# Local attention on one core: two slots for q and k, three for v and three for the output, and later requests for q and k

## The chip, the cores and the metric

The kernel runs on one core of one Trainium2 chip. The metric is the time of one execution on the device in microseconds (us). Before the change it is 954.06 us (median of 3 runs, 953.35 to 955.11); with the fourth run of the round that timed the change it is 954.44 us, and three later calls gave medians of 953.93 to 954.1 us for the same kernel. The profiler's span is about 1.8 us shorter than the time of the same execution (951.8 us beside 953.58 us).

Names in the profile: PE does the matrix products (PEld loads its weights), DVE and ACT do the vector and scalar work, GpSimd (POOL in the profile's lines) and SP issue transfers here. A DMA transfer is moved by the core's 16 DMA engines in packets, and it has landed when all of them have done their share.

## The reference

Attention in windows of 64 rows; a row attends to its own window alone.

```python
B, S, D, W = 4, 4096, 1536, 64
q_w = q.reshape(B, nw, W, D)            # k and v likewise; all float32
logits = einsum('bnwd,bnud->bnwu', q_w, k_w) * D ** -0.5
attn = exp(logits - logits.max(-1)); attn /= attn.sum(-1)
out = einsum('bnwu,bnud->bnwd', attn, v_w)
```

q, k, v and the output have 100.66 MB each, 402.7 MB in all. Every byte crosses between HBM and the core once.

## The kernel before

The 16,384 rows are cut into 32 units of 512 rows. The loads cast float32 to float16, and all loads and all stores but the last three small ones are issued by GpSimd on one queue. The last unit, unit 31, is cut into three parts (256, 128, 128 rows), so that the kernel ends with small pieces of work.

```python
AHEAD = 2
SLOTS = 4
...
units = [Unit(i * UR, [(0, 4, 2)]) for i in range(N - 1)]
units.append(Unit((N - 1) * UR, [(0, 2, 2), (2, 3, 1), (3, 4, 1)]))
inp = ctx.enter_context(tc.tile_pool(name="inp", bufs=AHEAD + 1))   # q, k, v: three slots each
outp = ctx.enter_context(tc.tile_pool(name="outp", bufs=2))
...
def load(u, i, name):
    ...
    nc.gpsimd.dma_start(out=dst, in_=rows(src, u.first[i], hi - lo, r))

def load_all(u):
    for i in range(len(u.parts)):
        for name in "qkv":
            load(u, i, name)
...
def values(u, i, h, et, last):
    if not hasattr(u, "o"):
        u.o = outp.tile([P, SLOTS, D], FP32, tag="out_sb", name="out_sb")
    ...                                  # row sums, products, each block scaled into u.o by ACT or DVE
            if last:
                nc.sync.dma_start(out=of[u.first[i] : u.first[i] + P, sl], in_=dst)

def store(u, i):
    lo, hi, R = u.parts[i]
    nc.gpsimd.dma_start(out=rows(of, u.first[i], hi - lo, R), in_=slots(u.o, lo, hi, R))

for ui, u in enumerate(units):
    if ui + AHEAD < N:
        load_all(units[ui + AHEAD])
    n = ui - 12
    if 1 <= n <= 15 and n != 8:          # 14 small loads that nothing uses
        w = 128 + 4 * n
        nc.gpsimd.dma_start(out=probe[:n, n, :w], in_=qf[0:n, :w])
    for i in range(len(u.parts)):
        last = ui == N - 1 and i == len(u.parts) - 1
        for h, et in scores(u, i):       # transposes of q and k, products, exp
            values(u, i, h, et, last)
        if not last:
            store(u, i)
```

A request waits in GpSimd's program order: for its slot to come free, and for one of eight transfers in flight to land. So a load that waits holds up the store behind it. In the timeline of before the first eight loads are issued by 6.4 us, and the ninth at 12.45 us, when the first has landed.

The softmax here doesn't subtract the row's maximum and nothing guards it: scores larger than these inputs give would overflow.

## Time and profile before

| | before |
|---|---|
| time, median of 3 runs | 954.06 us |
| span of the profiled execution | 951.8 us |
| PE, DVE, ACT busy | 70%, 45%, 45% |
| packet time on the 16 DMA engines, main queue | 100.6% of 16 spans |
| HBM traffic over the span | 423 GB/s |

The first lines are from the profile's page of before: DMA busy tenths in 40 slices, and the queues with packets, MB and the share of 16 engines' span that their packets took (a little over 100%, so the times of packets overlap).

```profile
DMA  9999999999999999999999999999999999999996
...
q0 software_dynamic: 27824, 250.96, 100.6%
q8 instruction: 44, 0.72, 0.3%
```

The DMA engines are full until the last slice.

The table by stretches of before follows, with busy time of each engine (and instructions), the granted clock of PE, the mean DMA share and GB/s.

```profile
core 0: us, PE busy (x) PEld busy (x) DVE busy (x) ACT busy (x) POOL busy (x), PEclk, DMA share, GB/s
150.00:440.00 290.00, 208.87 (x1712) 134.09 (x1711) 129.88 (x147) 132.82 (x188) 24.46 (x40) 0.87 1.02 270
...
930.00:935.00 5.00, 2.47 (x6) 0.80 (x6) 1.32 (x2) 1.37 (x2) 0.00 (x0) 0.50 0.70 297
935.00:940.00 5.00, 4.40 (x39) 3.09 (x37) 2.56 (x5) 1.61 (x3) 0.54 (x1) 0.72 0.54 229
940.00:945.00 5.00, 2.84 (x34) 2.03 (x34) 1.94 (x4) 3.35 (x6) 0.54 (x1) 1.00 0.63 259
945.00:951.80 6.80, 1.51 (x10) 0.57 (x10) 0.92 (x2) 2.00 (x5) 0.00 (x0) 0.72 0.49 188
```

In the middle the share is 1.02. From 930 us on it falls to about a half: the tail is not full. GpSimd's timeline of before (start, duration, what; in brackets the idle time before it and what ended it) shows why.

```profile
853.10 0.72 POOL L214 DMA_DIRECT2D out_dram<-out_sb  x1 [8.50 <-DVE out_sb L207]
858.98 0.54 POOL L79 DMA_DIRECT2D q<-in_q_dram  x1 [5.16 <-DMA k<-in_k_dram]
...
906.18 0.53 POOL L79 DMA_DIRECT2D v<-in_v_dram  x1 [3.11 <-DMA q<-in_q_dram]
910.13 0.71 POOL L214 DMA_DIRECT2D out_dram<-out_sb  x1 [3.43 <-ACT out_sb L205]
913.81 0.72 POOL L214 DMA_DIRECT2D out_dram<-out_sb  x1 [2.96 <-ACT xk L141]
937.60 0.54 POOL L214 DMA_DIRECT2D out_dram<-out_sb  x1 [23.07 <-DVE xq L141]
```

Between 859 and 906 us the nine small loads of unit 31 go out one by one. Unit 29's output was complete at 882.2 us (the end of DVE's last block), but its store stands behind them and goes out at 910.13. Unit 31 uses the same output slot as unit 29, so it has to wait. The list of waits of before (engine and line, what it waited for, us in total, times, longest):

```profile
DVE out_sb L207 <- DMA out_dram<-out_sb: 48.0, 19, 13.6
ACT out_sb L205 <- DMA out_dram<-out_sb: 30.0, 16, 14.1
```

The longest waits, 13.6 and 14.1 us, end at 931.8 us in the timeline, when that store has landed.

### The profile page before, as it was taken

What the parts mean: (1) busy time and instruction counts of PE and PEld (TensorE: products, weight loads), DVE (VectorE), ACT (ScalarE), POOL (GpSimd) and SP (SyncE); (2) the same over time, 40 slices, a digit from 0 to 9 for tenths busy, and PEclk for the clock granted to TensorE, in tenths of its full rate; (3) what the DMA queues carried; (4) which work ended last, traced back from release to release, by engine and by line L of the source; (5) the groups of instructions that cost most, each with busy time, mean ns of one, the idle gap of its engine ahead of it and who ended that gap; (6) DMA issues with size and microseconds to landing.
All of it is one profiled execution on the core that took longest, in us unless ns stands there. A gap on an engine that the chain in (4) does not pass through costs nothing.

```text
span 951.8 us, 12993 instructions
## 1 busy us (share of the span) xinstructions
PE 668.1 (70%) x5624; PEld 439.5 (46%) x5624; DVE 424.8 (45%) x489; ACT 431.0 (45%) x610; POOL 91.6 (10%) x154
## 2 busy tenths in 40 slices
PE   3777777768677677776676767767768668677644
PEld 3454445435454354553354544445445445344522
DVE  2554544544345443455434554434454345443422
ACT  2555544354444444444544345544354443454423
POOL 2101001010011000100011001100010101010000
PEclk9999989888799798899988889989798998898987
DMA  9999999999999999999999999999999999999996
GB/s 185 218 223 268 283 280 281 241 254 284 282 281 258 241 280 283 282 270 237 269 283 282 278 243 256 282 282 282 255 250 275 282 281 263 249 268 282 280 284 255
DMA packets 28313, 252.57 MB, mean 265 GB/s; under 512 B 2545, under 2 KB 2656, under 8 KB 12256
## 3 DMA queue, kind: packets, MB, share of 16 engines
q0 software_dynamic: 27824, 250.96, 100.6%
q8 instruction: 44, 0.72, 0.3%
q1 hardware_dynamic: 432, 0.79, 0.2%
q14 instruction: 13, 0.11, 0.0%
HBM read 302.07 MB, written 100.66 MB: 423 GB/s over the span
## 4 chain that ended last, share of the span: by engine, by line
DMA 63%; PE 13%; ACT 7%; another core or an unknown queue 7%; DVE 6%; issue 2%; POOL 1%; ACTq 0%; POOLq 0%; DVEq 0%
DMA out_dram<-out_sb 47%; DMA q<-in_q_dram 9%; PE o L199 8%; DMA k<-in_k_dram 7%; PE lt L148 3%; ACT out_sb L205 3%; DVE out_sb L207 3%; PE tp L135 3%; ACT et L174 2%; ACT xk L141 2%; DVE xk L141 2%; DVE xq L141 1%; ACT xq L141 0%; POOL out_dram L214 0%
## 5 line engine op out<-in xcount | busy, mean ns | idle before, releaser
L199 PE MATMUL o<-v,et 128*128 128x512 f16 x762 | 237.6, 420 | 91.2 <-ACT out_sb L205 86.8
L148 PE MATMUL lt<-xq,xk 128*128 128x256 f16 (+1 forms) x1536 | 232.6, 302 | 43.2 <-DVE xk L141 27.9
L207 DVE TENSOR_SCALAR out_sb<-o,rs 128x512 f32<-128x512 f32 x191 | 143.4, 751 | 197.7 <-PE o L199 149.7
L141 ACT COPY xk<-tp 128x1024 f16<-128x1024 f16 (+1 forms) x96 | 123.5, 1287 | 233.8 <-PE tp L135 233.8
L205 ACT ACTIVATE out_sb<-o,rs 128x512 f32<-128x512 f32 x193 | 132.6, 687 | 158.7 <-PE o L199 118.0
L141 DVE COPY xk<-tp 128x1024 f16<-128x1024 f16 (+1 forms) x97 | 123.3, 1271 | 178.6 <-PE tp L135 178.6
L148 PEld LDWEIGHTS <-xk 128*128 128x128 f16 x1536 | 151.9, 108 | 92.3 <-DVE xk L141 41.7
L135 PE MATMUL tp<-ident,k 128*128 128x128 f16 x1536 | 130.8, 239 | 66.4 <-DMA k<-in_k_dram 60.1
L199 PEld LDWEIGHTS <-et 128*128 128x128 f16 x762 | 74.0, 101 | 220.3 <-issue 183.3
L141 DVE COPY xq<-tp 128x1024 f16<-128x1024 f16 (+1 forms) x129 | 152.2, 1255 | 12.6 <-PE tp L135 12.5
L135 PEld LDWEIGHTS <-k 128*128 128x128 f16 x1536 | 113.3, 109 | 78.4 <-DMA k<-in_k_dram 68.3
L135 PE MATMUL tp<-ident,q 128*128 128x128 f16 x1536 | 103.7, 221 | 37.9 <-DVE xq L141 21.8
L141 ACT COPY xq<-tp 128x1024 f16<-128x1024 f16 x64 | 82.1, 1283 | 91.4 <-PE tp L135 91.4
L135 PEld LDWEIGHTS <-q 128*128 128x128 f16 x1536 | 93.2, 99 | 54.4 <-issue 34.6
L174 ACT ACTIVATE et<-lt,zeros 32x128 f16<-32x128 f32 (+1 forms) x256 | 91.6, 358 | 33.0 <-PE lt L148 27.4
L192 DVE RECIPROCAL rs<-sp 128x2 f32<-128x2 f32 (+1 forms) x65 | 10.7, 165 | 133.1 <-PE sp L187 133.1
L214 POOL DMA_DIRECT2D out_dram<-out_sb x33 | 23.8, 720 | 391.2 <-DVE out_sb L207 269.9
L187 PE MATMUL sp<-ones,et 128*128 128x1 f16 x254 | 16.4, 167 | 41.1 <-ACT et L174 41.1
L187 PEld LDWEIGHTS <-et 128*128 128x128 f16 x254 | 14.3, 102 | 61.8 <-ACT et L174 50.3
L79 POOL DMA_DIRECT2D v<-in_v_dram x34 | 23.6, 694 | 180.8 <-DMA out_dram<-out_sb 51.1
L79 POOL DMA_DIRECT2D q<-in_q_dram x34 | 18.6, 546 | 114.1 <-DMA probe<-in_q_dram 53.1
L79 POOL DMA_DIRECT2D k<-in_k_dram x34 | 18.6, 547 | 78.2 <-DMA k<-in_k_dram 37.2
(11 smaller groups left out, 10.1 us busy)
## 6 DMA issues: line engine op xcount, KB each, us to landing
out_dram<-out_sb POOLq DMA_DIRECT2D x31, 3072.0 KB, 44.0
q<-in_q_dram POOLq DMA_DIRECT2D x31, 1536.0 KB, 47.7
k<-in_k_dram POOLq DMA_DIRECT2D x31, 1536.0 KB, 50.8
v<-in_v_dram POOLq DMA_DIRECT2D x31, 1536.0 KB, 51.3
out_dram<-out_sb POOLq DMA_DIRECT2D x1, 1536.0 KB, 5.3
q<-in_q_dram POOLq DMA_DIRECT2D x1, 768.0 KB, 46.9
k<-in_k_dram POOLq DMA_DIRECT2D x1, 768.0 KB, 43.2
v<-in_v_dram POOLq DMA_DIRECT2D x1, 768.0 KB, 46.4
```

The lines of the kernel that those rows point to most:

```text
L79: nc.gpsimd.dma_start(out=dst, in_=rows(src, u.first[i], hi - lo, r))
L135: nc.tensor.transpose(tp[:, (c - c0) * R + r, j, :], src[:, lo + R * j + r, c * P : (c + 1) * P], ident,)
L141: copy(out=dst, in_=tp)
L148: nc.tensor.matmul(lts[h][:, r, :, :], lhsT=kc[:, r, h, :], rhs=qc[:, :, h, :], start=(c == 0 and r == 0), stop=(c == DC - 1), skip_group_ ...
L174: nc.scalar.activation(et[s, :, :, s], lts[h][s, :, :, s], EXP, bias=zeros[s], scale=scale)
L187: nc.tensor.matmul(sp[:, t, 0:1], lhsT=et[:, r, t, :], rhs=ones[:, 0:1], start=(r == 0), stop=(r == R - 1),)
L192: nc.vector.reciprocal(out=rs, in_=sp[:, :, 0])
L199: nc.tensor.matmul(o, lhsT=et[:, r, t, :], rhs=u.v[:, lo + R * h + r, sl], start=(r == 0), stop=(r == R - 1),)
L205: nc.scalar.activation(dst, o, COPY, bias=0.0, scale=rs[:, t : t + 1])
L207: nc.vector.tensor_scalar_mul(dst, o, scalar1=rs[:, t : t + 1])
L214: nc.gpsimd.dma_start(out=rows(of, u.first[i], hi - lo, R), in_=slots(u.o, lo, hi, R))
```

## The change

The intent is to repair the order and the slots within the same memory: q and k get two slots instead of three, v keeps three, the output gets three. q and k of unit u+2 are requested once unit u's score work is issued, and v of unit u+3 after unit u's store. The 14 probe loads are gone too.

```diff
-AHEAD = 2
 SLOTS = 4
-    inp = ctx.enter_context(tc.tile_pool(name="inp", bufs=AHEAD + 1))
+    qkp = ctx.enter_context(tc.tile_pool(name="qkp", bufs=2))
+    vp = ctx.enter_context(tc.tile_pool(name="vp", bufs=3))
-    outp = ctx.enter_context(tc.tile_pool(name="outp", bufs=2))
+    outp = ctx.enter_context(tc.tile_pool(name="outp", bufs=3))
 ... (load takes the pool by name; load_all takes a unit's number and names)
-    for u in units[1:AHEAD]:
-        load_all(u)
+    load_all(1, "qkv")
+    load_all(2, "v")
 ...
-    probe = consts.tile([16, 16, 192], FP32, name="probe")
     for ui, u in enumerate(units):
-        if ui + AHEAD < N:
-            load_all(units[ui + AHEAD])
-        n = ui - 12
-        if 1 <= n <= 15 and n != 8:
-            w = 128 + 4 * n
-            nc.gpsimd.dma_start(out=probe[:n, n, :w], in_=qf[0:n, :w])
         for i in range(len(u.parts)):
             last = ui == N - 1 and i == len(u.parts) - 1
-            for h, et in scores(u, i):
+            blocks = scores(u, i)
+            if i == 0:
+                load_all(ui + 2, "qk")
+            for h, et in blocks:
                 values(u, i, h, et, last)
             if not last:
                 store(u, i)
+        load_all(ui + 3, "v")
```

More of the change, by code (lines that the diff above doesn't have):

```diff
@@ L74, in load @@
         if not hasattr(u, name):
-            setattr(u, name, inp.tile([P, SLOTS, D], FP16, tag=name + "16", name=name + "16"))
+            pool = vp if name == "v" else qkp
+            setattr(u, name, pool.tile([P, SLOTS, D], FP16, tag=name + "16", name=name + "16"))
         src = {"q": qf, "k": kf, "v": vf}[name]
@@ L79, in load, with load_all @@
         nc.gpsimd.dma_start(out=dst, in_=rows(src, u.first[i], hi - lo, r))
-    def load_all(u):
-        for i in range(len(u.parts)):
-            for name in "qkv":
-                load(u, i, name)
-    load_all(units[0])
+    def load_all(ui, names):
+        if ui < N:
+            for i in range(len(units[ui].parts)):
+                for name in names:
+                    load(units[ui], i, name)
+    load_all(0, "qkv")
     ident = consts.tile([P, P], FP16, name="ident")
```

## The prediction

> **What bounds the kernel now: the DMA engines.** In the table by stretches the mean DMA share is 1.01 to 1.03 in every stretch from 2 to 910 us (1.02 over 150-440 and 440-870), while PE is busy 70%, DVE and ACT 45% on the page. HBM traffic is 402.7 MB; in the saturated middle I count 429.7 GB/s from the packet records, so a unit of 512 rows takes 29.3 us (an estimate: 12.58 MB over that rate). The Trainium skill, "DMA: Bandwidth & Descriptors", section "Where 436 GB/s comes from", gives 435 GB/s as the ceiling of the 16 engines; the trace agrees within 2%. So in the middle nothing can be won: no byte goes away but the probes' (14 loads, 78 KB).
>
> **Not bound by DMA: only the end.** In the timeline, unit 29's output is computed at 882.2 us, but its store is issued at 910.1: it stands on the GpSimd queue behind the nine small loads of unit 31, which go out about 7 us apart, each as an older transfer lands (eight in flight at most). With two output slots unit 31 needs the slot of unit 29: DVE and ACT wait from 918 to 931.8 us (13.6 and 14.1 us in the list of waits, released by that store's landing). Then the rest of unit 31 is computed with an almost empty DMA queue. DMA share: 0.70, 0.54, 0.63, 0.49 in 930-935, 935-940, 940-945, 945-951.8 us. Against 1.02 that is 9.4 us of lost DMA time.
>
> **What the change does.**
> - Output slots 2 to 3: unit 31 uses the slot of unit 28, free long before. The waits of DVE and ACT for a landed store (48.0 and 30.0 us in all) nearly vanish; before the tail they were off the critical path.
> - Order: q and k(u+2) go out after unit u's score work is issued, v(u+3) after its store. Unit 31's last loads precede the stores of units 29 and 30, so when its last k lands, about 22 us of stores (an estimate: 9.4 MB at 429.7 GB/s) are still to be moved, and its remaining compute (some 17 us by the old tail) runs under them.
> - Two slots: q(u+2) waits for unit u's transposes. I count about five to seven transfers of 7.3 us queued then, so the queue does not run dry. No gain, no loss.
> - Probes gone: at most 0.4 us of engine time.
> PE, DVE, ACT do the same instructions in the same order.
>
> **Sum.** Of 9.4 us lost in the tail, about 2.5 us stay (the last small stores take 2.3 us to land). Gain 7 us, plus 0.3 us for the probes: 954.06 - 7.3 = 946.8 us. The floor, 937 us of traffic + 2 before the first packet + 2 last landing + 2 between span and time, is 943. Predicted 946.8 us, 80% range 943.0 to 951.5. Chances: faster by over 2% 0.02, within 2% 0.96, slower 0.02.
>
> **Right if:** DMA share above 1.0 until about 5 us from the end; unit period still 29.3 us; no wait of DVE or ACT on a store's landing over 3 us; stores of units 29 and 30 issued after the last loads; span about 944.5 us; GpSimd's waits move from room in the queue to PE's transposes and the output.
>
> **Wrong if:** the late requests for q and k, with eight in flight as the limit, let the DMA run dry in each unit: 0.25 us per unit would cancel the gain. It shows as DMA share below 1.0 in the middle and PE waiting longer for k. Or if stores alone run slower than 430 GB/s.

## The result, and the profile after

The changed kernel takes 951.16 us (median of 4 runs, 950.88 to 951.59) beside 954.44 us. The ratio is 0.9967, with a 95% interval of 0.995 to 0.9984. Ratios are the mean time of one kernel's runs over that of the other's of the same rounds, so not quite the ratio of the medians. The change is faster by about 3 us; 7.3 us were predicted. The profiled spans are 949.6 and 951.8 us, a difference of 2.2 us.

The table by stretches of after:

```profile
150.00:440.00 290.00, 210.18 (x1734) 140.09 (x1731) 130.75 (x144) 130.12 (x182) 25.08 (x40) 0.86 1.02 269
...
930.00:935.00 5.00, 3.25 (x40) 2.22 (x39) 2.56 (x6) 2.12 (x5) 0.54 (x1) 1.00 0.95 403
935.00:940.00 5.00, 2.91 (x39) 2.27 (x39) 1.53 (x3) 3.04 (x6) 0.54 (x1) 1.00 0.91 379
940.00:945.00 5.00, 0.82 (x3) 0.10 (x1) 0.92 (x2) 1.38 (x2) 0.00 (x0) 0.79 0.67 268
945.00:949.60 4.60, 0.00 (x0) 0.00 (x0) 0.00 (x0) 0.00 (x0) 0.00 (x0) 0.50 0.13 51
```

The tail is repaired up to 940 us. The last row is the surprise. No compute is left at all, and yet there are 4.6 us with a DMA share of 0.13, on average the work of two engines out of sixteen. GpSimd's timeline of after shows the intended order, with the last load (k) before the stores of units 29 and 30:

```profile
907.51 0.53 POOL L80 DMA_DIRECT2D k<-in_k_dram  x1 [2.97 <-DMA v<-in_v_dram]
909.70 0.71 POOL L216 DMA_DIRECT2D out_dram<-out_sb  x1 [1.66 <-DVE rs L194]
919.59 0.72 POOL L216 DMA_DIRECT2D out_dram<-out_sb  x1 [9.18 <-DVE xq L143]
931.46 0.54 POOL L216 DMA_DIRECT2D out_dram<-out_sb  x1 [11.15 <-DVE xq L143]
936.70 0.54 POOL L216 DMA_DIRECT2D out_dram<-out_sb  x1 [4.69 <-ACT out_sb L207]
```

No wait of DVE or ACT on a store's landing is left in the list of waits of after. So the order and the waits came out as intended, and more than half of the gain did not.

**One transfer has sixteen ends.** The Trainium skill, "DMA: Bandwidth & Descriptors", section "Why a DMA increments its semaphore by 16 and not by 1", says that each of the 16 engines posts its own +1 when its share has landed, and that only the full 16 means that all data is there. The trace holds those sixteen times for every transfer of this kernel, so it tells how far the engines are apart. The times below, in us, were worked out from the trace's semaphore records; they are sorted, so a column is not always the same engine.

```
before, first load (q of unit 0):     10.8 10.9 10.9 11.0 11.1 11.2 11.2 11.2 11.3 11.3 11.3 11.4 11.5 11.5 11.8 12.2
before, store of unit 30:            931.0 931.1 931.5 931.5 931.9 933.4 933.9 936.4 937.6 937.6 937.8 937.9 938.2 938.3 938.4 939.0
before, next store (unit 31):        942.8 942.8 942.8 942.8 942.8 942.8 942.9 942.9 942.9 942.9 942.9 942.9 942.9 942.9 942.9 942.9
after,  store of unit 30:            931.3 931.4 932.3 933.3 933.5 934.6 934.9 935.0 936.8 937.1 938.2 938.2 938.9 939.8 940.2 940.3
after,  last store of all:           944.3 944.3 944.4 944.4 944.4 944.4 944.4 944.5 944.5 944.5 945.6 945.7 947.3 947.6 947.7 947.8
```

At the start the engines are 1.3 us apart. They drift, and at the end of the run they are 8 us (before) and 9 us (after) apart. In between the queue is full (a DMA share of 1.02 in the middle), and nothing brings them together. In the old tail the bubble did: the engines that were ahead waited for those behind, and the next store landed within 0.2 us. A good part of the old tail's low DMA share was the engines that were ahead, and their waiting costs nothing. This gives the following comparison, as seen by the first, the mean and the last of the sixteen landings:

| landing, us | before | after | difference |
|---|---|---|---|
| last store: first landing | 950.74 | 944.33 | -6.41 |
| last store: mean of 16 | 950.84 | 945.37 | -5.47 |
| last store: last landing | 950.93 | 947.76 | -3.17 |
| store of unit 30: first landing | 931.00 | 931.34 | +0.34 |
| store of unit 30: last landing | 938.99 | 940.32 | +1.33 |
| end of GpSimd's closing drain | 950.00 | 948.85 | |
| end of the span | 951.8 | 949.6 | -2.2 |

For the first engine the prediction was nearly right. The kernel ends with the last one. At the end, moreover, GpSimd's closing instruction (a drain) ended 1.1 us after the last landing of after; before, it ended 0.9 us ahead of it.

### The profile page after: what moved, and what is told of

It is laid out like the page before. It is cut to its first block, busy times and chain, and to the rows that moved or that the text cites. A ratio compares the mean times of both kernels' runs of the same rounds, so it can differ in the third digit from the quotient of the medians.

```text
span 949.6 us, 12981 instructions
## 1 busy us (share of the span) xinstructions
PE 667.9 (70%) x5624; PEld 444.9 (47%) x5624; DVE 425.4 (45%) x489; ACT 431.0 (45%) x610; POOL 84.2 (9%) x140
## 5 line engine op out<-in xcount | busy, mean ns | idle before, releaser
L201 PE MATMUL o<-v,et 128*128 128x512 f16 x762 | 224.3, 397 | 65.9 <-ACT out_sb L207 62.4
L150 PE MATMUL lt<-xq,xk 128*128 128x256 f16 (+1 forms) x1536 | 238.3, 307 | 41.4 <-DVE xk L143 26.2
L150 PEld LDWEIGHTS <-xk 128*128 128x128 f16 x1536 | 154.6, 110 | 92.6 <-DVE xk L143 39.4
L137 PE MATMUL tp<-ident,k 128*128 128x128 f16 x1536 | 137.5, 247 | 83.1 <-DMA k<-in_k_dram 80.0
L137 PEld LDWEIGHTS <-k 128*128 128x128 f16 x1536 | 119.3, 113 | 95.9 <-DMA k<-in_k_dram 86.6
L201 PEld LDWEIGHTS <-et 128*128 128x128 f16 x762 | 72.0, 98 | 186.7 <-issue 145.2
L189 PEld LDWEIGHTS <-et 128*128 128x128 f16 x254 | 13.7, 99 | 60.1 <-ACT et L176 50.3
```

The costliest lines, as they stand in the source:

```text
L137: nc.tensor.transpose(tp[:, (c - c0) * R + r, j, :], src[:, lo + R * j + r, c * P : (c + 1) * P], ident,)
L150: nc.tensor.matmul(lts[h][:, r, :, :], lhsT=kc[:, r, h, :], rhs=qc[:, :, h, :], start=(c == 0 and r == 0), stop=(c == DC - 1), skip_group_ ...
L189: nc.tensor.matmul(sp[:, t, 0:1], lhsT=et[:, r, t, :], rhs=ones[:, 0:1], start=(r == 0), stop=(r == R - 1),)
L201: nc.tensor.matmul(o, lhsT=et[:, r, t, :], rhs=u.v[:, lo + R * h + r, sl], start=(r == 0), stop=(r == R - 1),)
```

## The experiments

Three theories were held against each other. **A**: the time ends with the slowest of the 16 DMA engines; instruction fetches fall on some of the engines and make them lag; the drain adds 1 us. **B**: q and k with two slots are requested late, and the middle of the run loses some 4 us. **C**: the prediction's own view, that the tail is worth its mean DMA share. Every kernel below gave correct results.

### after_again: the changed kernel once more

No edit. This is the control.

> The changed kernel once more, as the control of this call. Theory A (the time ends with the slowest of the 16 DMA engines, which lags the fastest by some 9 us at the end; the old tail held only about 4.5 us of idle time of that engine, not the 9.4 us of the mean; and GpSimd's closing drain costs 1 us): 951.2 us, the 16 landings of one transfer spread by 8 to 9.5 us at unit 31's loads. Theory B (q and k with two slots are requested late and cost some 4 us in the middle): also 951.2 us, but the bursts of slow q and k packets of the first profile come again and the middle loses 3 us or more against the kernel without probes.

Measured: 951.08 us (5 runs, 950.38 to 951.86), ratio 0.9969. The spread of the sixteen landings was 9.7 us at unit 31's loads, just above A's 8 to 9.5. The bursts of slow q and k packets came again: 124 packets of over 0.96 us after the first 5 us, 141 in the first profile of the changed kernel, 23 in before. In the middle the changed kernel does lose something: the transfer in the same place of the sequence (the 120th data transfer, a load of unit 30) landed at 884.1 us on average over the engines (884.4 in the first profile), beside 883.5 us in the next experiment. That is 0.6 to 0.9 us, not 3 (on the slowest engine 1.3 to 1.6 us, about the 1.5 us that A allowed).

### no_probe: before without the 14 probe loads

```diff
-    probe = consts.tile([16, 16, 192], FP32, name="probe")
...
-        n = ui - 12
-        if 1 <= n <= 15 and n != 8:
-            w = 128 + 4 * n
-            nc.gpsimd.dma_start(out=probe[:n, n, :w], in_=qf[0:n, :w])
```

> The kernel before without the 14 probe loads, nothing else. Theory A: 953.3 to 954.2 us (the probes cost at most 1 us); its loads of unit 30 land within 1.5 us of those of the changed kernel on the slowest engine. Theory B: the same time, but its loads of unit 30 land 3 to 4 us ahead of the changed kernel's.

Measured: 953.62 us, ratio 0.9997 (0.9984 to 1.0009). The probes are worth 0.3 us at most, within the noise. Unit 30's store landed on the slowest engine at 939.05 us, beside 940.32 and 940.59 us in the two profiles of the changed kernel. The middle of the changed kernel costs its slowest engine 1.3 to 1.5 us. All profiles agree: 940.2 to 941.0 us in the five with the change's input slots and order, no added instructions and all larger stores on GpSimd (after, after_again, two_out, delay5, delay10), and 939.0 to 939.1 us in before, no_probe and tail_only.

### tail_only: only the order of the last unit's loads

This is no_probe with three input slots and two output slots as before. The nine loads of unit 31 go out after unit 29's store.

```diff
-        if ui + AHEAD < N:
+        if ui + AHEAD < N - 1:
             load_all(units[ui + AHEAD])
...
             if not last:
                 store(u, i)
+        if ui == N - 3:
+            load_all(units[N - 1])
```

> The kernel before without probes, still three input slots and two output slots; the only change is that unit 31's nine loads are requested after unit 29's store instead of before it. Theory A: the whole gain is the tail, so 950.0 to 951.7 us, like the changed kernel. Theory B: the same repair of the tail without the two slots' cost, so 946.5 to 948 us.

Measured: 950.55 us (950.46 to 950.56), ratio 0.9963. Three lines give the whole gain of the change, and 0.5 us more. So the gain is the tail, as A has it, and B as the main cause falls: without the two slots the time should have been 946.5 to 948 us. What is left of B is about 1 us in the middle. Its trace has 25 slow q and k packets, as few as before. So these come with the two slots for q and k or with the order of requests that goes with them; no run separates the two, and why they come is not known.

### sp_store: unit 31's two larger stores from SP

```diff
-        nc.gpsimd.dma_start(out=rows(of, u.first[i], hi - lo, R), in_=slots(u.o, lo, hi, R))
+        eng = nc.sync if u is units[-1] else nc.gpsimd
+        eng.dma_start(out=rows(of, u.first[i], hi - lo, R), in_=slots(u.o, lo, hi, R))
```

> The changed kernel with the first two stores of unit 31 issued from SP instead of GpSimd. Theory A: GpSimd's closing drain now waits for unit 30's store only and ends before the last landing, so the span loses about 1.0 us: 949.9 to 950.6 us. Theory B: no word on it; if the drain were not on the path, 951.2 us.

Measured: 950.71 us (950.0 to 951.12), a little above the range expected. In its profile the drain ended at 947.03 us, ahead of the last landing at 948.08, which itself was as in the control (948.00). The span was 949.0 us beside 949.5. The traces put the drain on the path of the changed kernel, with 0.5 us of the span here rather than 1.0. The medians differ by 0.4 us, which is not clear of noise, as the ranges overlap (950.38 to 951.86 us in the control); tail_sp below shows it more clearly.

### fetch: more instructions for PE

```diff
         (at the end of values)
+        if u not in units[-2:]:
+            for _ in range(44):
+                nc.tensor.matmul(sp[0:8, 0, 1:2], lhsT=ones[:, 0:8], rhs=ones[:, 0:1], start=True, stop=True)
```

The Trainium skill, "Runtime: NRT & Kernel Launch", section "Instruction fetch mechanics", says that an engine's instructions are refilled in blocks of 16 KiB (256 instructions) by DMA and that PE's memory holds 128 KiB, which is eight blocks; it calls the cost of a refill mostly hidden. The trace agrees with the blocks: 11,248 PE instructions (5,624 products and as many weight loads) make 44 packets of 16,384 bytes. Each took 0.88 to 0.98 us of one DMA engine, except for one of 1.35 us in after and one of 1.11 us in before. Their durations repeat roughly with period eight (893, 893, 949, 945, 936, 975, 960, 962 ns and again), as if eight fixed engines took them in turn.

> The changed kernel with 44 idle products (weights of 8 columns, one moving column, into an unused column of the sums' tile) after each block of units 0 to 29: 5,280 more PE instructions, so about 21 more instruction fetches of 16 KB beside the 44 of now, each some 0.94 us of one DMA engine. Theory A (instruction fetches fall on some of the engines, 8 by the repeating pattern of their durations, and make those lag): the spread of the 16 landings at unit 30's store grows from 9.0-9.7 us by about 2.5 us, to 11.5-12.5 us, the first landings hardly move, the time rises by 2 to 3 us to 953.2-954.2 us. Rival (the lag has another cause, such as slower engines): the spread stays 9 to 10 us and the time rises by at most 1.3 us (21 fetches over 16 engines).

Measured: 952.54 us, ratio 0.9981; that is 1.5 us above the control of the earlier call (before itself stood at 954.1 and 953.93 us in the two calls), less than the 2 to 3 us expected and a little over the rival's 1.3. By the time alone the run does not decide. Its page shows the fetches; the page of after has 44, 0.72 as that of before has.

```profile
q8 instruction: 64, 1.05, 0.4%
```

The spread at unit 30's store was 10.5 us, and 11.0 us at the loads before it. Its first landing stood still (931.2 us, beside 931.3 in after), and its last came later (941.7 beside 940.3). That is more than the 8.6 to 9.8 us at these two places in after, after_again, two_out, delay5 and delay10, which have the same order and 44 fetches, and less than expected. The next store of fetch landed in two groups, seven engines at 939.0 to 939.2, one at 940.7, eight at 943.7 to 945.3:

```
fetch, first store of unit 31:  939.0 939.0 939.0 939.1 939.1 939.2 939.2 940.7 943.7 944.2 944.4 944.5 944.7 945.0 945.0 945.3
```

A better measure than the spread is the distance between the mean of the eight later and the mean of the eight earlier landings at unit 30's store. If eight engines carry all the fetches, it should be near the number of fetches so far, divided by eight, times the mean time of one:

| run | fetches until then | fetches / 8 x mean time, us | later half minus earlier half, us |
|---|---|---|---|
| before | 43 | 5.05 | 5.52 |
| after | 44 | 5.20 | 5.40 |
| after_again | 44 | 5.19 | 5.48 |
| tail_only | 44 | 5.16 | 5.68 |
| delay10 | 43 | 5.04 | 4.91 |
| fetch | 64 | 7.50 | 8.05 |

Twenty more fetches added 2.3 us by this sum and 2.6 us as measured. Left out of the table are no_probe (5.52 us measured), two_out (5.13) and delay5 (5.80), with as many fetches as before, and sp_store, tail_sp and low8 (7.02, 9.01 and 5.67), where stores from SP ran beside unit 30's and its landings were 13 us apart. Sorting alone makes some distance: 0.46 us at the first load of before, with no fetch yet.

This place is not the only one. Over the 132 data transfers of before that landed by 930 us, the measured distance follows the sum of the fetches so far, divided by eight, with a slope of 1.02; in fetch the slope is 1.01 (both worked out from the trace's records). fetch_more, below, adds a third number of fetches at the same place. So the fetches are shown to make the distance between the halves. The rest, 1.4 to 5.7 us between the engines within a half at unit 30's store (before, after and fetch), is not explained. The trace does not number the engines, so which eight they are stays open. The sums would be the same for any number of engines up to eight; that they are eight is an inference from the period of the durations and from the late group of fetch, eight engines within 1.6 us of each other at both stores.

### fetch_more: twice as many again

The edit is that of fetch with `range(88)`.

> The kernel fetch with twice the idle products, so about 85 instruction fetches in place of 64 (44 in the changed kernel): at most 11 on one engine in place of 8 and 6. Theory A: the spread of the 16 landings at unit 30's store grows by 2 to 3 us over that of fetch (10.5 to 11.0), to 12.5 to 14 us, and the time by 2.0 to 2.8 us over that of fetch, to 954.5 to 955.3 us. Rival (fetches spread over all 16 engines, the lag has another cause): spread at most 11.5 us, 953.7 us.

Measured: 993.08 us, ratio 1.0408. The test failed: PE became the limit (80% busy, and the main queue's packets took 97.8% of 16 spans), which I had not foreseen. Its trace shows two things all the same. In its first half the DMA engines were still full (a share of 1.02 from 300 to 480 us), and there the lag grew with the fetches. At the 65th data transfer, which lands at 478 to 486 us in all four kernels:

| run | fetches until then | their time / 8, us | later half minus earlier half, us |
|---|---|---|---|
| before | 22 | 2.57 | 3.22 |
| after | 22 | 2.63 | 3.32 |
| fetch | 33 | 3.87 | 4.60 |
| fetch_more | 41 | 4.81 | 5.51 |

Then the distance fell, to 2.43 us at 602 us and 0.71 us at 662 us, and although the run had 85 fetches, the most of all, the sixteen landings of unit 30's store were only 0.2 us apart. Here the engines drifted apart while the queue was full, and came together once transfers waited for PE.

### delay5 and delay10: unit 31's stores later on purpose

Idle ACT copies ahead of unit 31's first output block, overwritten later; ten of them in delay10.

```diff
+        if u is units[-1] and i == 0:
+            for _ in range(5):
+                nc.scalar.activation(u.o[:, lo, 0:512], u.v[:, lo, 0:512], COPY, bias=0.0, scale=1.0)
         rs = rsp.tile([P, R], FP32, tag="rs", name="rs")
```

> The changed kernel with five idle ACT copies ahead of unit 31's first output block (overwritten later), so that all of unit 31's stores are issued some 2.5 to 3.5 us later. Theory A (the slowest DMA engine is still busy with earlier transfers then, and only it counts): nothing or little, 951.0 to 951.8 us, though the engines that are ahead stand idle 2.5 to 3.5 us longer. Theory C (the tail is worth its mean DMA share, as the prediction had it): 953.6 to 954.6 us.

Measured for delay5: 951.74 us (951.47 to 952.3), 0.6 to 0.7 us above the changed kernel. GpSimd's timeline of delay5 has the two stores of unit 31 3.8 us later than in after (931.46 and 936.70 there) and 2.7 us later than in after_again (932.56 and 937.80), and the first of the table's rows shows the emptier DMA engines (0.95 in after).

```profile
935.26 0.54 POOL L219 DMA_DIRECT2D out_dram<-out_sb  x1 [13.79 <-DVE xq L143]
940.54 0.54 POOL L219 DMA_DIRECT2D out_dram<-out_sb  x1 [4.74 <-ACT out_sb L210]
```

```profile
930.00:935.00 5.00, 3.73 (x19) 2.04 (x19) 1.80 (x3) 2.45 (x4) 0.00 (x0) 0.66 0.74 315
...
945.00:949.90 4.90, 0.25 (x1) 0.00 (x0) 0.08 (x1) 0.69 (x1) 0.00 (x0) 0.52 0.45 168
```

The first engine landed the first of these stores 3.7 us later (940.43 beside 936.77 us), the last engine 0.6 us later (944.64 beside 944.05). The end followed the last one. C had asked for 953.6 us or more. This is the clearest of the runs: 2.7 to 3.8 us of delay that the mean DMA share counts in full cost 0.6 us. The last store of all landed within 0.3 us on all engines here (3.4 us in after), so the slack of the slowest one was just used up.

> The same with ten copies, some 6 us. Theory A: the slack of the slowest engine (about 3.5 us between the issue and the landing of the last stores) is used up, the rest shows: 952.8 to 954.0 us. Theory C: 956.5 to 957.5 us.

Measured for delay10: 953.54 us (952.06 to 954.42), within A's range for a delay that goes beyond the slack. Its profile fell in the fastest of the five runs (952.06 us, span 950.3), so its traces explain that run and not the median.

### two_out: the new order with two output slots

```diff
-    outp = ctx.enter_context(tc.tile_pool(name="outp", bufs=3))
+    outp = ctx.enter_context(tc.tile_pool(name="outp", bufs=2))
```

> The changed kernel with two output slots in place of three (new order of requests, two slots for q and k, three for v). Theory A: unit 31 waits for unit 29's store to land (933 us) before it can write, its compute of some 17 us then is the end of the path: 952.5 to 953.8 us; the wait of ACT and DVE on a store's landing comes back in the tail with 5 to 8 us. If the third output slot were of no account, 951.1 us.

Measured: 954.3 us, ratio 0.9997, half a microsecond above the range expected. The whole gain is gone, so within the new order the third output slot carries it. The list of waits of two_out shows the wait back in the tail, one of ACT and one of DVE:

```profile
ACT out_sb L207 <- DMA out_dram<-out_sb: 6.4, 1, 6.4
DVE out_sb L209 <- DMA out_dram<-out_sb: 5.9, 1, 5.9
```

### low8: the last big store on eight engines

The first store of unit 31 goes out as 16 pieces of 8 partitions from SP. The Trainium skill, "DMA: Bandwidth & Descriptors", section "Why a DMA increments its semaphore by 16 and not by 1", has such pieces on the lowest-numbered eight engines. The trace has nine semaphore updates for each piece and not sixteen, which fits eight engines and one early write; no run here shows which engines they are.

```diff
+        if u is units[-1] and i == 0:
+            for p in range(0, P, 8):
+                nc.sync.dma_start(out=dst[p : p + 8], in_=src[p : p + 8])
```

> Like sp_store, but the first store of unit 31 (1.5 MB) goes out as 16 pieces of 8 partitions each from SP, so that 8 of the 16 engines carry all of it. If all engines were equal, the 8 would end 3.6 us later: 954.3 us against the 950.7 of sp_store. Theory A (some engines lag 9 us, others not at all): it depends on which 8 they are; if they are the ones ahead, 948 to 950 us; if they are the late ones, up to 954.5 us.

Measured: 956.85 us, slower than every expectation. The packets of these pieces took 864 ns on average where those of the same 12,288 bytes in sp_store took 464 ns, so the pieces were slow in themselves, for a reason that no run separates, and SP's later stores were held back too (the last one was issued at 951.9 us). The run says nothing about which engines lag. It is inconclusive.

### tail_sp: tail_only with unit 31's two larger stores from SP

The edits of tail_only and sp_store together.

> The kernel tail_only with unit 31's two larger stores issued from SP. Theory A: the GpSimd drain, which ended 1.5 us after the last landing in tail_only, goes off the path; the end is then set by the last landing: 949.0 to 949.9 us, the fastest so far.

Measured: 949.35 us (5 runs, 948.67 to 949.66), ratio 0.9944 (0.9931 to 0.9958). This is the fastest version; it beats before by 0.6% and the changed kernel by about 1.7 us, with fewer edits. In its profile the span is 947.9 us, the drain ends at 946.67 us and the last landing at 946.98. In tail_only these were 948.03 and 946.53 us: the last landing did not come earlier, the drain went off the path, and the time fell by 1.2 us (tail_only took 950.46 to 950.56 us).

## Why the prediction was right or wrong

- **What bounds the kernel: right.** The DMA share is 1.02 in the middle before and after. The Trainium skill, "DMA: Bandwidth & Descriptors", section "Where 436 GB/s comes from", gives 435 GB/s as the ceiling of the 16 SBUF ports that these engines move data through; the prediction's count from the packet records in the middle was 429.7. That count is of float32 bytes at HBM; in the table by stretches, where the loads count as the float16 bytes that arrive, it is 269 to 270 GB/s. So the nearness of the two figures does not show that this ceiling is what binds.
- **Where the gain is: right.** Only the tail. tail_only shows it: three changed lines of order give 950.55 us, the full gain.
- **"The waits for a landed store nearly vanish", "Unit 31's last loads precede the stores of units 29 and 30": right**, seen in the timeline and the waits of after; two_out brings the wait and the old time back. The sign "DMA share above 1.0 until about 5 us from the end" did not come: it was 0.95 and 0.91 from 930 to 940 us, when the engines that were ahead had less left to do.
- **"Against 1.02 that is 9.4 us of lost DMA time ... about 2.5 us stay. Gain 7 us": wrong.** This is the step that failed, a term of the sum that was mis-sized. The share is a mean over 16 engines, and they end a transfer 8 us apart. From the landing of unit 30's store to the end of the last store, the slowest engine took 11.94 us before (950.93 - 938.99) and 7.44 us after (947.76 - 940.32), so the repair was worth 4.50 us where the prediction had 6.9. delay5 shows directly that the mean share is the wrong measure.
- **"Two slots ... No gain, no loss": nearly right.** The queue did not run dry, but the middle cost the slowest engine 1.33 us in the profiled pair, with bursts of slow q and k packets; against no_probe and tail_only it was 1.2 to 1.5 us.
- **"2 between span and time" and 2 for the last landing: incomplete.** GpSimd's drain, which the sum did not have, ended 1.1 us after the last landing in after. From the last landing to the end of the span it is 0.9 us before and 1.85 us after, a loss of 0.96 us. sp_store took the drain off the path and won 0.4 us of time, within the noise; tail_sp won 1.2 us over tail_only, clear of it.
- **"Probes gone: at most 0.4 us": right**; no_probe won 0.3 us by medians, not clear of noise.

The sum for the profiled pair: 4.50 - 1.33 - 0.96 = 2.21 us, the measured difference of the spans. (It must close, being three pieces of one axis; what the experiments add is what each piece is.) Against the prediction's 7.2 us (6.9 and 0.3 for the probes) 2.4 us are missing in the tail, 1.3 in the middle, 1.0 at the drain, and the probes' 0.3. The medians differ by more than this pair, by 3.3 us in the first rounds and 2.85 us in the later ones: the profiled run of before was one of its faster (953.58 us), that of after one of its slower (951.38 us).

The floor of 943 us in the prediction was probably too low for the same reason, which no run shows: it divided all traffic over 16 equal engines. The best version, at 949.35 us, ends with an engine that is late.

## What to carry to other kernels

A mean DMA share can hide that the 16 engines finish apart, by 8 to 9 us here: before costing a bubble in a queue that is otherwise full, look at the sixteen landings of one transfer, and cost the bubble for the latest engine alone. In a kernel with one long queue, look at the last few requests in program order, since moving one group of small loads behind one store was worth as much as a new set of slots. Let the queue whose engine has a long closing instruction finish its last transfers early: it was worth 1.2 us in tail_sp.

## What the Trainium skill lacked or had wrong

- "Runtime: NRT & Kernel Launch", "Instruction fetch mechanics", calls a refill mostly hidden. It does not say that a refill takes time of the DMA engines that carry the data. "DMA: Bandwidth & Descriptors" does put refills on a queue row of the same 16 engines, but neither page says what that costs: 44 packets of 16 KB at 0.94 us here, 41 us of engine time, apparently on eight of the sixteen engines; the later eight were 4.9 to 5.7 us behind in the runs of the table with 43 or 44 fetches, 8.05 us with 64.
- "DMA: Bandwidth & Descriptors" says that the engines finish independently and calls two of them usually slower, but not that the engines drift apart over a queue that is never empty: from 1.3 us at the first load to 8 or 9 us after 930 us, and 0.2 us again after the queue has run dry. Whether those two have a part in it stays open, as the trace does not number the engines.
- No page that I found tells that GpSimd's closing drain ends some 2.6 us after its own last transfer has landed (946.23 to 948.85 us in after; 3.0 us in before).
